# Ratings inside the last projection groups, weights behind the gather indices, and six filler matmuls

## The chip, the cores and the metric

One core of a Trainium2 chip runs the whole program. The metric is the device time of one execution in microseconds. Before the change it is 911.22 us, the median of 3 runs (910.05 to 912.13).

## What is computed

One decoder layer for 512 prompt tokens and 8 sample tokens (520 rows of 1024 columns, float32). Three sublayers follow one another, each with a residual and a layer normalization:

```python
hp = layer_norm(ALPHA * hp + mix_p, ln1_g[l], ln1_b[l])                      # linear attention + latent attention
hp = layer_norm(ALPHA * hp + cross_attention(hp, mk_p, mv_p, w_xq[l], w_xo[l]), ln2_g[l], ln2_b[l])
hp = layer_norm(ALPHA * hp + hier_moe(hp, *moe_w), ln3_g[l], ln3_b[l])

def hier_moe(h, w_grp, b_grp, w_rtr, b_rtr, w_e_gate, w_e_up, w_e_down):
    grp_logits = jnp.einsum('td,dg->tg', t, w_grp)            # 4 groups
    g_idx = jnp.argmax(grp_logits + b_grp, axis=-1)
    e_logits = jnp.einsum('td,de->te', t, w_rtr)              # 32 experts, 8 in a group
    _, top_i = lax.top_k(in_grp + in_bias, TOP_K_IN_GROUP)    # two experts of the token's group
    ...
    for e in range(N_EXPERTS):
        he = jax.nn.silu(t @ w_e_gate[e]) * (t @ w_e_up[e])
        y = y + gates[:, e:e + 1] * (he @ w_e_down[e])
```

The change lies between the second sublayer's output projection (`w_xo`) and the first expert pair of the third.

## The kernel before, in words

**Rows and names.** The 520 rows are tiles 0 to 3 of 128 rows and tile 4, the 8 sample rows. `out_proj("wxo", ...)` multiplies by `w_xo` in four column quarters q; `natural` (L422 on) runs, for each q, first the sample rows, then tiles 0 to 3. One tile of one quarter is a *group* of 24 matmuls (8 k times the three products of a split float32). After a group `put` adds the residual and takes statistics on VectorE; after q = 3 `put` calls `finish(t)`, which normalizes the tile (`normalize`: aggregate, square root on ScalarE, reciprocal, one 1024-column subtract-and-multiply), stores it to `h2d` in DRAM from the SP queue, and enters the tile's *rating* as a stream.

**Rating.** `rate(t)` transposes the normalized tile (8 PE transposes, L223, into `psm`), copies the two halves out on ScalarE and VectorE, and after a pause multiplies by the router weights (16 PE instructions into `pss`), then adds biases on VectorE.

**Order of PE.** `keep_in_program_order` pins TensorE to the order in which the text emits matmuls. That order comes from `Streams.run`: the live generators are sorted by priority; the first whose due time has come runs to its next `yield`. Time there is `PE.now`, the planner's own estimate: 0.123 for a matmul of a projection group (2.94 for a group), 0.11 for a transpose, 0.06 for a router matmul. A rating has priority -1, so it goes first whenever its due time is reached at a `yield`. The projection yields once at the end of each group. The order of VectorE, ScalarE, SP and POOL is drawn up by a list scheduler from priorities (program order) and readiness; `tc.high_priority(offset=...)` moves instructions forward in it.

**The step to the experts.** When the last group is out, `second` closes the pool of the split weights and opens `arena_l` in its place; `prefetch` then issues one DMA of 512 KB (`in_we`) for every free block of 1024 columns. A block comes free again when `gate_up` has used it (`drop`, after every second k); the first two that come free go to `sums` for other use. After the ratings of all five tiles VectorE finds group and two experts for each token (`first_max`), PE counts ranks (`pp`, then `placed`), and VectorE makes the row index of each expert slot (`ixg`, L1834 and L1835). POOL gathers the rows of the first two expert pairs by it (indirect DMA from `h2d`, L1841). Behind the gathers stand `grank` (rank in the group) and, in `weigh`, the gate weights and the group places; `weigh` is called inside `gate_up(0)`. `warm(2)` puts two 512-column float32 matmuls on PE ahead of `turn(0)`, which transposes the gathered rows; `gate_up(0)` follows, then the 15 other pairs. Each expert has 3 MB of weights, 100.7 MB in all.

Of the kernel before, what the change touches and what calls it, by code (L numbers as in the profile page):

```python
# [16 lines left out]
AF = mybir.ActivationFunctionType  # L17
OP = mybir.AluOpType
AX = mybir.AxisListType
# [16 lines left out]
PRIO = 300  # L36
# [262 lines left out]
def tile_hybrid_decoder_step(ctx: ExitStack, tc: tile.TileContext, a):  # L299
    nc = tc.nc  # L300
    PE = Tensor(tc, nc.tensor)
    Q = Loads(PE, nc.sync)
    V, S, G = Engine(PE, nc.vector, 1.05e-3), Engine(PE, nc.scalar, 0.83e-3), Engine(PE, nc.gpsimd, 2.25e-3)
# [42 lines left out]
    streams = Streams(PE)  # L346
# [69 lines left out]
    def natural(name, parts, x, xs, put, ks=range(8), tiles=range(4), need=None):  # L416

        for q in range(parts):  # L420
            ws = {}
            for k in ks:  # L422
                if k // 4 not in ws:
                    ws[k // 4] = yield from weight(a[name][q, k // 4], xs is not None)
            done.add((name, q))
            if xs is not None:
                if need and q == 0:
                    yield need(4)
                ps = pd()
                for i, k in enumerate(ks):  # L430
                    PE.matmul(ps[32 * (i % 4):32 * (i % 4) + NS, :256], xs[:, k],
                              ws[k // 4][2][:, (k % 4) * 256:(k % 4) * 256 + 256], start=i < 4, stop=i >= 4,
                              abreast=4)
                raws.extend(w[2] for w in ws.values())
                put(4, q, ps)
            for t in tiles:
                if need and q == 0:
                    yield need(t)
                ps = pd()
                for i, k in enumerate(ks):  # L440
                    w = [v[:, (k % 4) * 256:(k % 4) * 256 + 256] for v in ws[k // 4][:2]]
                    mm3(ps[:, :256], *x(k, t), *w, i == 0, i == 7)
                put(t, q, ps)
                yield PE.now
            for w in ws.values():
                release(w)
# [897 lines left out]
    def normalize(t, parts):  # L1344
        y, n = res[t], tiles5[t][1]
        mv, rs = moments(t, parts)
        V.tensor_scalar(y[:n], y[:n], mv[:n, 0:1], rs[:n], op0=OP.subtract, op1=OP.mult)
# [304 lines left out]
    def rate(t):  # L1652

        o, n = tiles5[t]
        slots = moe["xt"].slots
        if not slots:
            yield lambda: slots
        h2T = slots.pop(0)
        for c in range(2):
            ps = pm()  # L1660
            for k in range(4):
                f = 4 * c + k
                PE.transpose(ps[:, k * 128:k * 128 + n], res[t][:n, f * 128:(f + 1) * 128], ident[:n, :n])
            to, p3 = h2T[:, 4 * c:4 * c + 4, :n], ps.rearrange("p (k n) -> p k n", k=4)[:, :, :n]
            if c:
                V.tensor_copy(to, p3)
            else:
                S.copy(to, p3)
        yield PE.ready()
        ps = ps_()  # L1670
        for k in range(8):
            PE.matmul(ps[:n, :36], h2T[:, k, :n], moe["wrt"][:, k], start=k == 0, stop=k == 7)
        V.tensor_add(biased[:n, t], ps[:n, :36], moe["bias2"][:n])
        V.tensor_add(logits[:n, t], ps[:n, :36], moe["bias"][:n])
        slots.append(h2T)
        done.add(("rated", t))
# [3 lines left out]
    def second():  # L1680
        yield after("cross queries")

        def finish(t):
            o, n = tiles5[t]
            normalize(t, 4)
            Q.dma_start(h2d[o:o + n, :], res[t][:n])
            streams.add(rate(t), -1, PE.now + 3.8)

        yield from out_proj("wxo", columns2(hh, hl), xs, range(8), finish, lambda t: crossed)
        AF_.free(raws, xs)  # L1690
        pre.close()
        late = ctx.enter_context(tc.tile_pool(name="late", bufs=1, side="right", reuse_waits="tile"))
        AF_.more.more = Arena(late.tile([128, COLS_L], F32, name="arena_l"), COLS_L)
        moer = ctx.enter_context(tc.tile_pool(name="moer", bufs=1, side="right", reuse_waits="tile"))
        AM = Arena(moer.tile([128, COLS_M], F32R, name="arena_m"), COLS_M)
        moe["oh"], moe["yh"] = Ring(AM, 2, GC), Ring(AM, 2, 2, D)
        prefetch()
        yield after(*(("rated", t) for t in range(5)))
        AF_.free(res)
        moe["sums"] = [AF_.get(D) for _ in range(2)]  # L1700
        prefetch()
# [43 lines left out]
    BC = [128, 5]  # L1745
# [34 lines left out]
    el = logits[:, :, 4:36]  # L1780
    eb4 = biased[:, :, 4:36].rearrange("p t (g e) -> p t g e", g=4)
    pp = pm()
    OH = []
    og4 = None
    for k in range(2):
        o = first_max(eb4, 4, 8)
        if og4 is None:
            og = first_max(biased[:, :, None, 0:4], 1, 4)
            og4 = og.rearrange("p t o g -> p t (o g)")[:, :, :, None].to_broadcast(BC + [4, 8])
# [12 lines left out]
    pos = pp[:, :160].rearrange("p (t e) -> p t e", t=5)  # L1802
    rank = R(2, keep=True)
    VAL, RR = [R(2, 4, 16, dt=BF) for _ in range(2)], []
    t32 = R(32)
    ps = pm()
# [25 lines left out]
        placed(ps, k, val, k == 0, k == 1)  # L1832
    ixg = M([16], I32, keep=True)
    V.tensor_scalar(ixg, ps[:, :16], BIG, None, op0=OP.add)  # L1834
    V.tensor_tensor(ixg, ixg, ps[:, 16:32], op=OP.add)  # L1835


    xgs, ohr, yhr, iota = (moe[n] for n in ("xg", "oh", "yh", "iota"))
# [9 lines left out]
    for pr in range(2):  # L1848
# [1 line left out]


    grank = R()
    V.tensor_tensor(t32.rearrange("p t (g e) -> p t g e", g=4), og4, pos.rearrange("p t (g e) -> p t g e", g=4),
                    op=OP.mult)
    V.reduce_sum(grank, t32, axis=AX.X)
    V.tensor_scalar(grank, grank, 0.5, None, op0=OP.mult)

    OHS, YH, HT = {}, {}, {}

    def warm(n):  # L1860

        ps = px()
        for _ in range(n):
            PE.matmul(ps, ident, iota[:, :512], start=True, stop=True)
# [134 lines left out]
        Q.dma_start(v, a["lnr"][i:i + 1].to_broadcast([128, D]))  # L1999
        last.append(v)  # L2000

    warm(2)
    turn(0)
    vv, gate, gslot, over = R(2, keep=True), M([16], keep=True), M([16], keep=True), M([1], I32, 1, True)
    gix = M([2, 4], I32, keep=True)
# [1 line left out]
    def weigh():  # L2007

        gl_ = logits[:, :, 0:4]
        m0, gs, pg, ge = R(), R(), R(), R(4)  # L2010
        V.reduce_max(m0, gl_, axis=AX.X)
        V.tensor_tensor(ge, gl_, m0[:, :, None].to_broadcast(BC + [4]), op=OP.subtract)
        S.activation(ge, ge, AF.Exp)
        V.reduce_sum(gs, ge, axis=AX.X)
        V.reciprocal(gs, gs)
        V.tensor_mul(ge, ge, og.rearrange("p t o g -> p t (o g)"))
        V.reduce_sum(pg, ge, axis=AX.X)
        V.tensor_mul(pg, pg, gs)
        for k in range(2):
            V.tensor_mul(t32, OH[k], el)  # L2020
            V.reduce_sum(vv[:, :, k], t32, axis=AX.X)
        V.reduce_max(m0, vv, axis=AX.X)
        V.tensor_tensor(vv, vv, m0[:, :, None].to_broadcast(BC + [2]), op=OP.subtract)
        S.activation(vv, vv, AF.Exp)
        V.reduce_sum(gs, vv, axis=AX.X)
        V.reciprocal(gs, gs)
        V.tensor_mul(gs, gs, pg)
        V.tensor_tensor(vv, vv, gs[:, :, None].to_broadcast(BC + [2]), op=OP.mult)
        vp = R(2, 4, dt=BF)
        V.tensor_scalar(vp[:, :, :, 3], grank[:, :, None].to_broadcast(BC + [2]), 255.0, -256.0, op0=OP.min, op1=OP.add)  # L2030
        rest = vv
# [6 lines left out]
        ps = ps_()  # L2038
# [210 lines left out]
```

## Time and profile before

| | us |
|---|---|
| median of 3 runs | 911.22 |
| the profiled execution's own time | 907.26 |
| its span | 905.5 |
| last projection quarter and ratings | 597.2 to 623.1 |
| choice of experts, to the row index | 623.2 to 632.4 |
| first expert pair's first matmul | 639.6 |
| DMA queue full | from 648 to 870 |
| end of the last expert and output | 870 to 905.5 |

The times inside the span come from one profiled execution, counted from its start. It is 3.96 us under the median of the runs. A row of the timeline merges neighbouring instructions of one form: its first number is the start, its second the time from the first start to the last end. PE is the matmul engine, PEld its weight loads, DVE VectorE, ACT ScalarE, POOL GpSimd, SPq the SP queue's DMA issues.

### The profile page before, as it was taken

What the parts mean: (1) busy time and instruction counts of PE and PEld (TensorE: products, weight loads), DVE (VectorE), ACT (ScalarE), POOL (GpSimd) and SP (SyncE); (2) the same over time, 40 slices, a digit from 0 to 9 for tenths busy, and PEclk for the clock granted to TensorE, in tenths of its full rate; (3) what the DMA queues carried; (4) which work ended last, traced back from release to release, by engine and by line L of the source; (5) the groups of instructions that cost most, each with busy time, mean ns of one, the idle gap of its engine ahead of it and who ended that gap; (6) DMA issues with size and microseconds to landing.
All of it is one profiled execution on the core that took longest, in us unless ns stands there. A gap on an engine that the chain in (4) does not pass through costs nothing.

```text
span 905.5 us, 17155 instructions
## 1 busy us (share of the span) xinstructions
PE 820.4 (91%) x6767; PEld 575.3 (64%) x6767; DVE 485.7 (54%) x1079; ACT 294.4 (33%) x616; POOL 87.5 (10%) x88
## 2 busy tenths in 40 slices
PE   6999989999997898999989989996899989989982
PEld 6998556666875786898768965995343434334331
DVE  5565356675557554533651675567453834625635
ACT  5422334352632433420442342121232403313311
POOL 4100101111320000000000001000310210200100
PEclk9999999999997987999979999998899999989997
DMA  7922696766793576688867346228699999999950
GB/s 265 310 80 79 178 281 203 247 196 230 231 350 132 192 256 233 228 307 318 268 218 278 98 162 209 84 107 313 209 409 411 412 409 410 408 409 409 409 210 24
DMA packets 83960, 230.43 MB, mean 254 GB/s; under 512 B 12482, under 2 KB 32988, under 8 KB 83492
## 3 DMA queue, kind: packets, MB, share of 16 engines
q1 hardware_dynamic: 74660, 203.98, 62.7%
q0 software_dynamic: 9216, 25.31, 8.0%
q8 instruction: 55, 0.90, 0.4%
q14 instruction: 29, 0.24, 0.1%
HBM read 223.11 MB, written 14.39 MB: 262 GB/s over the span
## 4 chain that ended last, share of the span: by engine, by line
PE 62%; DMA 22%; DVE 8%; ACT 3%; issue 2%; SPq 2%; POOL 0%; POOLq 0%; ACTq 0%; DVEq 0%
PE psd L219 33%; DMA arena_f<-in_we 10%; PE psm L219 9%; PE psx L219 9%; PE pss L219 7%; DVE arena_f L200 5%; DMA arena_d<-in_we 4%; PE psm L223 3%; DMA arena_l<-in_we 2%; DVE arena_r L200 2%; DMA arena_f<-in_latT 2%; ACT arena_f L200 2%; ACT arena_r L200 1%; SPq L239 1%; DMA arena_f<-in_wuq 1%
## 5 line engine op out<-in xcount | busy, mean ns | idle before, releaser
L219 PE MATMUL psd<-arena_r 128*128 128x256 f32 (+1 forms) x2208 | 295.9, 293 | 9.0 <-ACT arena_r L200 5.6
L219 PEld LDWEIGHTS psd<-arena_r 128*128 128x128 f32 x2208 | 281.7, 198 | 21.5 <-issue 9.3
L219 PE MATMUL psx<-arena_f 96*32 96x256 f32 (+1 forms) x728 | 132.7, 495 | 2.2 <-DMA arena_f<-in_latT 1.9
L200 DVE TENSOR_TENSOR arena_r<-arena_f,arena_r 128x1024 fp32r<-128x1024 f32 (+3 forms) x71 | 83.0, 1173 | 77.3 <-ACT arena_r L200 71.7
L200 ACT CAST arena_r<-arena_f 128x1024 fp32r<-128x1024 f32 (+3 forms) x73 | 71.2, 977 | 159.2 <-PE psd L219 118.7
L219 PE MATMUL psm<-arena_f 64*32 64x32 f32 (+10 forms) x1394 | 87.1, 282 | 14.4 <-DVE arena_f L200 9.4
L219 PE MATMUL pss<-arena_f 128*8 128x256 f32 (+5 forms) x466 | 92.3, 466 | 1.3 <-ACT arena_f L200 0.7
L219 PEld LDWEIGHTS psx<-arena_f 96*32 96x32 f32 (+1 forms) x728 | 43.9, 125 | 68.5 <-issue 51.9
L223 PE MATMUL psm<-cst,arena_f 128*128 128x128 f32 (+2 forms) x393 | 59.9, 280 | 19.8 <-DVE arena_f L200 5.4
L219 PEld LDWEIGHTS psm<-arena_f 64*32 64x32 f32 (+6 forms) x1384 | 47.6, 123 | 46.2 <-issue 22.5
L223 PEld LDWEIGHTS psm<-cst,arena_f 128*128 128x128 f32 (+2 forms) x393 | 44.0, 148 | 44.1 <-issue 20.4
L200 DVE TENSOR_TENSOR arena_f<-arena_f 128x1024 f32<-128x1024 f32 (+6 forms) x72 | 57.2, 827 | 7.5 <-ACT arena_f L200 3.6
L219 PEld LDWEIGHTS pss<-arena_f 128*8 128x8 f32 (+3 forms) x456 | 30.3, 121 | 37.8 <-issue 26.7
L200 DVE TENSOR_TENSOR arena_f<-arena_f,psx 128x256 f32<-128x256 f32 (+1 forms) x17 | 7.4, 432 | 86.9 <-ACT arena_f L200 86.9
L638 POOL DMA_INDIRECT arena_f<-in_latN,ixn x32 | 34.3, 1073 | 189.9 <-PE psm L219 176.2
L200 DVE SCALAR_TENSOR_TENSOR arena_f<-arena_f,psd 128x256 f32<-128x256 f32 (+2 forms) x60 | 28.6, 489 | 43.9 <-PE psd L219 34.6
L1841 POOL DMA_INDIRECT arena_f<-h2d,arena_s x24 | 26.2, 1092 | 220.8 <-PE psm L223 123.6
L200 ACT ACTIVATE arena_f<-psx 128x256 f32<-128x256 f32 x16 | 6.1, 384 | 122.8 <-PE psx L219 117.5
L219 PE MATMUL psx<-arena_d,arena_f 128*64 128x512 f32 x76 | 37.1, 676 | 9.4 <-DMA arena_d<-in_we 9.4
L219 PE MATMUL pss<-arena_l,arena_f 128*64 128x512 f32 x92 | 43.2, 593 | 0.0
L219 PE MATMUL psx<-arena_l,arena_f 128*64 128x512 f32 x92 | 35.7, 596 | 5.2 <-DMA arena_l<-in_we 5.2
L200 DVE SCALAR_TENSOR_TENSOR arena_m<-pss,arena_s,arena_m 128x512 fp32r<-128x512 f32 x32 | 23.7, 750 | 29.7 <-ACT arena_m L200 29.7
(212 smaller groups left out, 919.8 us busy)
## 6 DMA issues: line engine op xcount, KB each, us to landing
arena_f<-in_we SPq DMA_DIRECT2D x120, 512.0 KB, 10.6
arena_l<-in_we SPq DMA_DIRECT2D x46, 512.0 KB, 10.8
arena_f<-in_latT SPq DMA_DIRECT2D x128, 144.0 KB, 2.9
arena_d<-in_we SPq DMA_DIRECT2D x26, 512.0 KB, 11.1
arena_f<-in_wout SPq DMA_DIRECT2D x16, 512.0 KB, 5.5
arena_f<-in_wxq SPq DMA_DIRECT2D x16, 512.0 KB, 5.4
arena_f<-in_memKT SPq DMA_DIRECT2D x16, 512.0 KB, 5.3
arena_f<-in_memV SPq DMA_DIRECT2D x16, 512.0 KB, 5.2
```

The lines of the kernel that those rows point to most:

```text
L200: return f(out, *args, **kw)
L219: return self.queue(self.eng.matmul(out, lhsT, rhs, **kw))
L223: return self.queue(self.eng.transpose(out, src, ident))
L239: return self.eng.dma_start(out, src)
L638: G.indirect_dma_start(out=out, out_offset=None, in_=src, in_offset=bass.IndirectOffsetOnAxis(ap=ix, axis=0))
L1841: G.indirect_dma_start(out=out, out_offset=None, in_=h2d, in_offset=bass.IndirectOffsetOnAxis(ap=ix, axis=0), bounds_check=NT - 1, oob_is_ ...
```

## The change

It has four parts. The projection yields once more, in the middle of each group of the last quarter. A rating becomes due 2.8 instead of 3.8 planner-us after `finish`, and the normalization of tile 3 gets a higher priority. `grank` and the first part of `weigh` are put, on VectorE, behind the second `ixg` instruction (`issue_after`: order of issue alone, no wait). The fillers ahead of `turn(0)` become six.

```diff
@@ natural @@
                 for i, k in enumerate(ks):
+                    if name == "wxo" and q == 3 and i == 4:
+                        yield PE.now
                     w = [v[:, (k % 4) * 256:(k % 4) * 256 + 256] for v in ws[k // 4][:2]]
@@ second @@
         def finish(t):
             o, n = tiles5[t]
-            normalize(t, 4)
+            with tc.high_priority(offset=PRIO if t == 3 else 0):
+                normalize(t, 4)
             Q.dma_start(h2d[o:o + n, :], res[t][:n])
-            streams.add(rate(t), -1, PE.now + 3.8)
+            streams.add(rate(t), -1, PE.now + 2.8)
@@ the row index @@
-    V.tensor_tensor(ixg, ixg, ps[:, 16:32], op=OP.add)
+    indices = V.tensor_tensor(ixg, ixg, ps[:, 16:32], op=OP.add).ins
@@ grank @@
-    V.tensor_tensor(t32..., og4, pos..., op=OP.mult)
-    V.reduce_sum(grank, t32, axis=AX.X)
-    V.tensor_scalar(grank, grank, 0.5, None, op0=OP.mult)
+    with tc.issue_after(indices):
+        V.tensor_tensor(t32..., og4, pos..., op=OP.mult)
+        V.reduce_sum(grank, t32, axis=AX.X)
+        V.tensor_scalar(grank, grank, 0.5, None, op0=OP.mult)
@@ ahead of turn(0) @@
-    warm(2)
+    warm(6)
     turn(0)
@@ weigh @@
-        V.reduce_max(m0, gl_, axis=AX.X)
-        V.tensor_tensor(ge, gl_, m0[:, :, None].to_broadcast(BC + [4]), op=OP.subtract)
...
-        V.tensor_tensor(vv, vv, gs[:, :, None].to_broadcast(BC + [2]), op=OP.mult)
+        with tc.issue_after(indices):
+            V.reduce_max(m0, gl_, axis=AX.X)
+            V.tensor_tensor(ge, gl_, m0[:, :, None].to_broadcast(BC + [4]), op=OP.subtract)
...
+            V.tensor_tensor(vv, vv, gs[:, :, None].to_broadcast(BC + [2]), op=OP.mult)
```

## Rows read from the trace of the kernel before

**Rows 1.** Stretches: length, busy us (instructions) of PE, PEld, DVE, ACT, POOL; PEclk, DMA share, GB/s

```profile
634.00:636.00 2.00, 1.49 (x2) 0.00 (x0) 1.66 (x9) 0.21 (x1) 1.70 (x2) 0.51 0.44 133
636.00:638.00 2.00, 0.00 (x0) 0.00 (x0) 1.23 (x8) 0.00 (x0) 0.37 (x1) 1.00 0.57 172
...
640.00:644.00 4.00, 4.00 (x14) 1.13 (x12) 2.00 (x9) 2.18 (x3) 0.65 (x1) 0.65 0.25 68
...
660.00:870.00 210.00, 194.40 (x891) 81.01 (x887) 108.72 (x191) 60.33 (x123) 25.76 (x22) 0.98 1.03 410
```

**Rows 2.** SP queue, timeline 612 to 650: weight and tile DMAs as they are issued

```profile
615.12 0.83 SPq L239 DMA_DIRECT2D arena_l<-in_we  x2
619.38 0.33 SPq L239 DMA_DIRECT2D h2d<-arena_f  x1
...
644.83 4.24 SPq L239 DMA_DIRECT2D arena_f<-in_we  x6
```

**Rows 3.** PE timeline 597 to 640: last quarter, ratings, ranks, fillers, first rows

```profile
598.13 6.01 PE L219 MATMUL psd<-arena_r 128*128 128x256 f32 x48
604.08 1.83 PE L223 MATMUL psm<-cst,arena_f 8*128 8x8 f32 x16
...
614.93 1.87 PE L219 MATMUL pss<-arena_s,arena_f 128*128 128x36 f32 x16
616.63 1.07 PE L223 MATMUL psm<-cst,arena_f 128*128 128x128 f32 x8
...
621.16 1.98 PE L219 MATMUL pss<-arena_s,arena_f 128*128 128x36 f32 x16 [0.29 <-ACT arena_f L200]
...
631.22 0.56 PE L219 MATMUL psm<-arena_f,arena_s 128*64 128x32 bf16 x10 [0.55 <-DVE arena_s L200]
631.71 3.78 PE L219 MATMUL psx<-arena_f,cst 128*128 128x512 f32 x4
638.32 1.06 PE L223 MATMUL psm<-cst,arena_f 128*128 128x128 f32 x8 [2.83 <-DMA arena_f<-h2d,arena_s]
```

**Rows 4.** DVE timeline 599 to 619: sample rows normalized, then tile 3

```profile
601.31 0.42 DVE L200 SCALAR_TENSOR_TENSOR arena_f<-arena_f,psd 128x256 f32<-128x256 f32 x1
...
602.54 0.80 DVE L200 TENSOR_SCALAR arena_f<-arena_f,mv,lrs 8x1024 f32<-8x1024 f32 x1
...
615.12 0.42 DVE L200 SCALAR_TENSOR_TENSOR arena_f<-arena_f,psd 128x256 f32<-128x256 f32 x1 [1.97 <-PE psd L219]
615.58 0.43 DVE L200 BATCH_NORM_STATS2 arena_s<-arena_f 128x6 f32<-128x256 f32 x1
...
618.54 0.81 DVE L200 TENSOR_SCALAR arena_f<-arena_f,mv,lrs 128x1024 f32<-128x1024 f32 x1
```

**Rows 5.** DVE timeline 631 to 635: around the row index

```profile
631.98 0.32 DVE L200 TENSOR_TENSOR arena_f<-arena_s 128x160 f32<-128x160 bf16 x1
632.22 0.17 DVE L200 TENSOR_TENSOR arena_s<-arena_s,psm 128x16 int32<-128x16 int32 x1
...
632.64 1.48 DVE L200 TENSOR_TENSOR arena_f<-arena_f 128x1280 bf16<-128x1280 f32 x1
```

**Rows 6.** POOL timeline 633 to 637, and the chain's wait for the first gather

```profile
633.15 1.92 POOL L1841 DMA_INDIRECT arena_f<-h2d,arena_s  x1 [74.60 <-DMA arena_f<-in_we]
635.38 0.99 POOL L1841 DMA_INDIRECT arena_f<-h2d,arena_s  x1 [0.30 <-issue]
...
633.15 5.04 DMA arena_f<-h2d,arena_s
```

**Rows 7.** All row gathers from `h2d`, the view of that tile

```profile
DMA to landing us min/median/max: 2.9/7.4/10.4
```

**Rows 8.** PEld timeline: some weight loads of the first `gate_up`

```profile
639.56 0.29 PEld L219 LDWEIGHTS psx<-arena_f 128*64 128x64 f32 x4 [0.41 <-ACT arena_f L200]
...
642.17 0.24 PEld L219 LDWEIGHTS psx<-arena_f 128*64 128x64 f32 x2 [0.62 <-issue]
...
643.35 0.14 PEld L219 LDWEIGHTS psx<-arena_f 128*64 128x64 f32 x2 [0.29 <-issue]
643.77 0.14 PEld L219 LDWEIGHTS psx<-arena_f 128*64 128x64 f32 x2 [0.29 <-issue]
```

More of the change, by code (lines that the diff above doesn't have):

```diff
@@ L1852, in tile_hybrid_decoder_step @@
     grank = R()
-    V.tensor_tensor(t32.rearrange("p t (g e) -> p t g e", g=4), og4, pos.rearrange("p t (g e) -> p t g e", g=4),
-                    op=OP.mult)
-    V.reduce_sum(grank, t32, axis=AX.X)
-    V.tensor_scalar(grank, grank, 0.5, None, op0=OP.mult)
+    with tc.issue_after(indices):
+        V.tensor_tensor(t32.rearrange("p t (g e) -> p t g e", g=4), og4, pos.rearrange("p t (g e) -> p t g e", g=4),
+                        op=OP.mult)
+        V.reduce_sum(grank, t32, axis=AX.X)
+        V.tensor_scalar(grank, grank, 0.5, None, op0=OP.mult)
     OHS, YH, HT = {}, {}, {}
@@ L2010, in weigh @@
         m0, gs, pg, ge = R(), R(), R(), R(4)
-        V.reduce_max(m0, gl_, axis=AX.X)
-        V.tensor_tensor(ge, gl_, m0[:, :, None].to_broadcast(BC + [4]), op=OP.subtract)
[L2013 to L2027, printed above, removed]
-        V.tensor_tensor(vv, vv, gs[:, :, None].to_broadcast(BC + [2]), op=OP.mult)
+        with tc.issue_after(indices):
+            V.reduce_max(m0, gl_, axis=AX.X)
+            V.tensor_tensor(ge, gl_, m0[:, :, None].to_broadcast(BC + [4]), op=OP.subtract)
+            S.activation(ge, ge, AF.Exp)
+            V.reduce_sum(gs, ge, axis=AX.X)
+            V.reciprocal(gs, gs)
+            V.tensor_mul(ge, ge, og.rearrange("p t o g -> p t (o g)"))
+            V.reduce_sum(pg, ge, axis=AX.X)
+            V.tensor_mul(pg, pg, gs)
+            for k in range(2):
+                V.tensor_mul(t32, OH[k], el)
+                V.reduce_sum(vv[:, :, k], t32, axis=AX.X)
+            V.reduce_max(m0, vv, axis=AX.X)
+            V.tensor_tensor(vv, vv, m0[:, :, None].to_broadcast(BC + [2]), op=OP.subtract)
+            S.activation(vv, vv, AF.Exp)
+            V.reduce_sum(gs, vv, axis=AX.X)
+            V.reciprocal(gs, gs)
+            V.tensor_mul(gs, gs, pg)
+            V.tensor_tensor(vv, vv, gs[:, :, None].to_broadcast(BC + [2]), op=OP.mult)
         vp = R(2, 4, dt=BF)
```

## The prediction, made before the changed kernel had run

> **What bounds the kernel now.** I read the stretches first, then the SP queue, then back through PE and VectorE. From 660 to 870 us the DMA share is 1.03 at 410 GB/s [rows 1]: the expert weights arrive as fast as the queue moves them, and PE waits for them at the end. The last expert's work after 870 is the same in both kernels. So the end of the run is fixed by when that stream gets going, and the reader is to look at where it last paused. Between 634 and 648 it did: 133, 172 and 68 GB/s [rows 1]. SP's next weight block leaves at 644.83 us [rows 2], because every free block is filled and another comes free only when the first `gate_up` has used k = 0 to 3 (the first two blocks to come free go to `sums`). What moves that 644.83 moves the end of the run by as much; what does not move it is worth nothing.
>
> The chain to 644.83 runs: last router product of tile 3 on PE, to 623.14; VectorE's choice of experts, with PE's rank products to 631.78; fillers to 635.49; the first gathered rows' transposes from 638.32 [rows 3], released by the gather that POOL started at 633.15 and that landed 5.04 us later [rows 6]; `gate_up` from 639.56 [rows 8].
>
> **Part 1, ratings among the groups.** PE is nearly full from 598.13 to 623.14 [rows 3], so an exchange of order there can win only PE's idle time, two pauses of 0.29 like the one in the row of 621.16 and little else. What counts is whether the new order makes PE wait. I followed the planner by hand, with its own prices: a group is 2.94, and `finish(4)` comes with the sample rows, at time S. Before, the sample rating is due at S + 3.8, which falls inside the second group, so its transposes stand behind tiles 0 and 1; the rows show them there, at 604.08. Now it is due at S + 2.8, and tile 0's group ends at S + 2.94: its transposes stand right behind tile 0. Continuing, I get the order: tile 0, transposes of 4, tile 1, transposes of 0, half of tile 2, router product of 4, transposes of 1, the other half, products of 0 and 1, tile 3, transposes of 2 and 3, products of 2 and 3.
>
> On the chip tile 0 ends at 598.13 + 2.98 = 601.1 (two groups take 5.95 from start to start). The sample rows are normalized only at 602.54 + 0.80 = 603.34 [rows 4]. PE's order is pinned, so it stands 2.3 us, and all groups behind it wait. From there: transposes of 4 to 603.85, tile 1 to 606.8, transposes of 0 (0.95; eight of them take 1.07 with the tail) to 607.75, half a group to 609.25, product of 4 to 610.05 (0.8, an estimate between nothing and the 1.7 of a full one), transposes of 1 to 611.0, half a group to 612.5, two products at 1.7 (614.93 to 616.63) to 615.9, tile 3 to 618.9. Transposes of 2 need 0.95. Those of tile 3 need its normalization: 0.42 + 0.43 + 0.81 [rows 4] and three small steps of about 0.3 with their handovers, 2.6 in all; before it took from 615.12 to 619.35, since other work stood between, and the raised priority takes that away. So they start at 621.5, 622.45 ends them, products of 2 and 3 end at 626.0. Against 623.14 that is **2.9 us later**. The bounds: 2.3 less if the sample rows' wait is not there, up to 1.1 under 623.14 if PE never waits.
>
> The pool of split weights closes when tile 3's group is out, so the fill of `arena_l` starts at 618.9 instead of 615.12 [rows 2]. Its blocks must land before the stream's restart, which leaves room (see the rivals).
>
> **Part 2, work behind the index.** Small VectorE steps of `grank` and `weigh` stood among the choice of experts. One is a 0.32 step at 631.98 between the two index instructions; without it the index ends some 0.2 sooner [rows 5]. Ahead of 631.78 the moved ones are mostly small steps that fill latencies between dependent instructions; I give them 0.2 (nothing to 0.5). They reappear behind the index. They are about a dozen steps of the size of 0.17 to 0.32 [rows 5], 2 to 3 us in all. Their readers are PE's gate products, which stand behind `gate_up(0)`; VectorE was busy 1.23 of 2 us from 636 and 2.00 of 4 from 640 [rows 1], so their cost is nothing. Without that cover it would be the 2 to 3 us. ScalarE's two exponentials move with their inputs.
>
> A gather started at 633.15 took 1.92, the next 0.99 [rows 6]; the long one stood beside a 1.48 us VectorE instruction with both inputs in SBUF, from 632.64 to 634.12 [rows 5], and ended 0.95 after it. The Trainium skill (SBUF — State Buffer, section Who interferes with whom) says that such an instruction and a GpSimd instruction that reads SBUF exclude each other, whoever comes first for its whole length. The trace agrees for one instruction; the change puts a row of them exactly behind the index, and by that rule POOL could lose to several in turn and the gather land 2 to 3 us later than with one, at 643 instead of 640.7 below, which would give 914.3 instead of 912.9. The row shows POOL losing once only, and I go by the row.
>
> **Part 3, six fillers.** Two fillers are four PE records. At half clock a record takes 0.87 (639.56 to 642.17 in three steps), at full clock 0.42 (643.35 to 643.77) [rows 8]. Six fillers are twelve: 5.0 us at full clock, 10.4 at half. The granted clock read 0.51 until 636 and 1.00 from there, some 4.3 us after the first filler at 631.71 [rows 1, 3]; then it fell again, and the first `gate_up` ran at 0.65 on average. With 4.3 us at half clock (4.9 records) and 7.1 records at 0.42 the six take 7.3. `turn(0)` stands behind them on PE. They start when the rank products end: 631.78 + 2.9 - 0.2 = 634.5, and end at 641.8, against transposes at 638.32 before. The gather: index at 632.39 + 2.9 - 0.4 = 634.9, POOL 0.76 later (632.39 to 633.15), so 635.7, and landing 5.04 later, 640.7: hidden. The fillers are late next, by about a microsecond.
>
> In return PE stays at full clock: from `turn` to `gate_up` 1.24 as before (its transposes already took 1.06, like the 1.07 at 616.63), then k = 0 to 3, eight steps of 0.43 and the issue, 3.6 instead of 5.27 (639.56 to 644.83).
>
> **The sum.** 641.8 + 1.24 + 3.6 = 646.6 against 644.83: 1.7 us later. The profiled execution's own 907.26 becomes 909.0. The runs' median stands 3.96 above that execution; I put the same shift on it: **912.9**. That is 0.19%, so still "no change" if 0.2% (1.8 us) is about what a measurement of this kernel can tell.
>
> **The rivals.**
>
> *The sample rows' wait does not bite* (the change's first part does nothing): the normalization of 4 is drawn up earlier, or its transposes land behind tile 1 after all. Then 2.3 come off: 910.6. For it: VectorE took up tile 0's residual at 601.31, ahead of the last step of tile 4's normalization [rows 4], an order that a scheduler could turn round. Against: the program up to there is unchanged, and so is what the scheduler sees.
>
> *The ratings do what they say* (faster): PE never waits and the last product ends 1.1 sooner, 622.0. Rank products end at 630.5, fillers at 637.8, `gate_up` starts at 639.0, blocks are issued at 642.6: 2.2 sooner, 909.0. For it: without waits PE's work from 598.13 would allow it. Against: tile 3's normalization alone needs 2.6 behind its group, then 0.95 + 1.7 + 1.7 or more follow.
>
> *The gather lands behind the fillers* (slower). The fill starts 3.8 later and lasts longer into the gather; in a full queue a gather takes 7.4 from issue to landing, alone 2.9 [rows 7]. From 635.7 that is 638.6 to 643.1. It decides from 641.8 on; at 643.1 it adds 1.3: 914.2. For it: the fill before still moved 133 GB/s after 634 [rows 1], with its start at 615.12, and the first gather lost 0.93 (1.92 less 0.99) beside VectorE [rows 6]. Against: SP stood from 615.95 to 619.38 behind tile 3's store [rows 2], and part of that goes.
>
> **How the numbers follow.** Forecast 0.43 (own range 911.6 to 914.2: with the clock rising 1.4 sooner or later the fillers move by 0.7, the small estimates by as much again). No wait 0.21, faster 0.20, late gather 0.16. The forecast's case lies to 0.25 within 0.2% and to 0.18 above it; the no-wait case is within; the late gather above but for 0.02. Faster 0.21, same 0.47, slower 0.32. The range leaves out half of the faster case and the far end of the late gather: 908.6 to 914.8.
>
> **What would show it.** In the trace of the changed kernel: transposes of 4 behind one group, with a PE pause of about 2 us ended by VectorE; tile 3's transposes ahead of the product of tile 2, waiting for VectorE; twelve filler records with the later ones at 0.42; the first `gate_up` at clock 1.00 throughout; SP's first block after the pause near 646.6. If that block comes before 644.8 and the run is not faster, the claim that the stream's restart sets the end is wrong. If PE does not pause at tile 4, the planner was followed wrongly.

## The result, and the profile after

| | before | after |
|---|---|---|
| median of 13 runs each, us | 911.22 | 916.05 |
| ratio, with its 95% interval | 1 | 1.0057 (1.0036 to 1.0077) |
| profiled execution: time; span | 907.26; 905.5 | 914.27; 912.4 |

The changed kernel is about 5 us slower. The forecast was 912.9 with a range up to 914.8: the direction was right, but the time lies above the range.

The PE timeline of the changed kernel (start, us from the first start to the last end, what; in brackets idle time ahead and what ended it) answers to [rows 3]:

```profile
599.67 3.13 PE L219 MATMUL psd<-arena_r 128*128 128x256 f32 x24
605.02 0.63 PE L223 MATMUL psm<-cst,arena_f 8*128 8x8 f32 x8 [2.22 <-DVE lrs L200]
605.58 4.43 PE L219 MATMUL psd<-arena_r 128*128 128x256 f32 x24
...
618.95 3.11 PE L219 MATMUL psd<-arena_r 128*128 128x256 f32 x24
621.90 1.03 PE L223 MATMUL psm<-cst,arena_f 128*128 128x128 f32 x8
624.88 1.06 PE L223 MATMUL psm<-cst,arena_f 128*128 128x128 f32 x8 [1.95 <-DVE arena_f L200]
625.78 5.41 PE L219 MATMUL pss<-arena_s,arena_f 128*128 128x36 f32 x32
...
639.12 0.56 PE L219 MATMUL psm<-arena_f,arena_s 128*64 128x32 bf16 x10 [0.55 <-DVE arena_s L200]
639.62 7.81 PE L219 MATMUL psx<-arena_f,cst 128*128 128x512 f32 x12
647.26 1.04 PE L223 MATMUL psm<-cst,arena_f 128*128 128x128 f32 x8
648.47 7.09 PE L219 MATMUL psx<-arena_f 128*64 128x512 f32 x32 [0.17 <-ACT arena_f L200]
```

The order is the one that the prediction drew up by hand, with its two pauses: 2.22 us ahead of tile 4's transposes and 1.95 us ahead of tile 3's. What the prediction did not have is in the third row: tile 1's group, the same 24 matmuls as tile 0's two rows above, takes 4.43 us instead of 3.13. The two last router products take 5.41; in [rows 3] one takes 1.87 to 1.98. The stretches show the granted clock beside it (columns as in [rows 1]):

```profile
600.00:606.00 6.00, 3.78 (x35) 3.58 (x34) 5.52 (x15) 0.77 (x3) 0.00 (x0) 1.00 0.57 180
606.00:610.00 4.00, 4.00 (x24) 4.00 (x23) 0.00 (x0) 0.00 (x0) 0.00 (x0) 0.61 0.34 134
606.00:607.00 1.00, 1.00 (x10) 1.00 (x9) 0.00 (x0) 0.00 (x0) 0.00 (x0) 0.96 0.43 164
607.00:608.00 1.00, 1.00 (x7) 1.00 (x6) 0.00 (x0) 0.00 (x0) 0.00 (x0) 0.50 0.91 369
610.00:618.00 8.00, 8.00 (x81) 7.80 (x79) 4.83 (x14) 1.68 (x4) 0.00 (x0) 0.98 0.18 68
...
622.00:626.00 4.00, 2.05 (x20) 1.84 (x18) 2.55 (x7) 1.27 (x3) 0.00 (x0) 1.00 0.83 278
626.00:632.00 6.00, 5.20 (x31) 5.06 (x30) 1.74 (x8) 1.47 (x2) 0.00 (x0) 0.62 0.94 326
```

The reader is to look at PEclk: 1.00 in the stretch that holds a pause, 0.61 and 0.62 in the stretch behind it. At a granted clock of 1.00 TensorE runs at 2.4 GHz, at 0.50 at 1.2. The fall comes a little behind the pause: PE is at work again from 605.02, the clock still reads 0.96 from 606 to 607, and 0.50 in the microsecond after that. By these rows each pause is paid twice, first by its length and then by slow work behind it; the experiments put this to the test.

SP's queue, answering to [rows 2]:

```profile
652.15 4.32 SPq L239 DMA_DIRECT2D arena_f<-in_we  x6
```

The first weight block after the pause leaves at 652.15 instead of 644.83, 7.32 later. In this execution everything ahead of the change already ran 1.54 later (tile 0's last group starts at 599.67, not 598.13). I therefore count from the start of that group, here S: block at S + 52.48, before at S + 46.70, so 5.78 later by the change. The span grew by 6.9, which is the 7.32 less the 0.4 by which the stretch from that block to the last `gate_up` was shorter.

POOL, answering to [rows 6]:

```profile
640.88 1.20 POOL L1844 DMA_INDIRECT arena_f<-h2d,arena_s  x1 [80.79 <-DMA arena_f<-in_we]
```

The first gather holds POOL for 1.20 us instead of 1.92. Nothing on PE waits for its rows: `turn` stands right behind the fillers.

### The profile page after: what moved, and what is told of

Read it like the earlier page. It is cut to its first block, busy times and chain, and to the rows that moved or that the text cites. A ratio compares the mean times of both kernels' runs of the same rounds, so it can differ in the third digit from the quotient of the medians.

```text
span 912.4 us, 17171 instructions
## 1 busy us (share of the span) xinstructions
PE 831.9 (91%) x6775; PEld 591.2 (65%) x6775; DVE 486.2 (53%) x1079; ACT 294.2 (32%) x616; POOL 85.8 (9%) x88
## 4 chain that ended last, share of the span: by engine, by line
PE 62%; DMA 23%; DVE 9%; ACT 3%; issue 2%; SPq 1%; POOL 0%; POOLq 0%; DVEq 0%; ACTq 0%
PE psd L219 33%; DMA arena_f<-in_we 11%; PE psm L219 9%; PE psx L219 9%; PE pss L219 7%; DVE arena_f L200 5%; PE psm L223 4%; DMA arena_d<-in_we 3%; DMA arena_l<-in_we 2%; DVE arena_r L200 2%; ACT arena_f L200 2%; DMA arena_f<-in_latT 1%; ACT arena_r L200 1%; DMA arena_f<-in_wuq 1%; DVE arena_s L200 1%
## 5 line engine op out<-in xcount | busy, mean ns | idle before, releaser
L219 PE MATMUL psd<-arena_r 128*128 128x256 f32 (+1 forms) x2208 | 301.8, 296 | 8.8 <-ACT arena_r L200 5.6
L219 PEld LDWEIGHTS psd<-arena_r 128*128 128x128 f32 x2208 | 286.8, 202 | 21.6 <-issue 8.9
L219 PE MATMUL psm<-arena_f 64*32 64x32 f32 (+10 forms) x1394 | 89.1, 282 | 10.8 <-DVE arena_f L200 7.8
L219 PEld LDWEIGHTS psx<-arena_f 96*32 96x32 f32 (+1 forms) x728 | 45.9, 124 | 66.1 <-issue 46.3
L219 PEld LDWEIGHTS psm<-arena_f 64*32 64x32 f32 (+6 forms) x1384 | 49.7, 124 | 42.7 <-issue 22.2
```

The source lines that it names most:

```text
L219: return self.queue(self.eng.matmul(out, lhsT, rhs, **kw))
```

## The experiments

W is the end of the last rank product on PE (639.68 in the changed kernel, 631.78 before). From S to the last router product, from there to W, and from W to SP's first block are the three pieces of the chain. As in the prediction, the first part is the yield in mid-group, the earlier ratings and tile 3's priority together, the second the steps behind the index, the third the six filler pairs. "SP's block" is the first weight block after the pause of the stream. Theory: the pauses of the first part cost their length and the half clock behind them. Rivals: the fillers or the moved steps cost it, or the groups are slow for another reason.

S itself falls between 598.13 and 609.54 in the fourteen profiled executions, though the program ahead of it is the same in all of them. That is more than any of the changes is worth, so the pieces of the chain, each of one execution, are read from S or W, and the intervals of the ratios, some 2 to 3 us to each side, often hold 1 as well as the ratio that was expected.

**1. The first part undone.**

```diff
-                    if name == "wxo" and q == 3 and i == 4:
-                        yield PE.now
...
-            with tc.high_priority(offset=PRIO if t == 3 else 0):
-                normalize(t, 4)
+            normalize(t, 4)
...
-            streams.add(rate(t), -1, PE.now + 2.8)
+            streams.add(rate(t), -1, PE.now + 3.8)
```

> The changed kernel with its first part undone: ratings are queued as in the kernel before; the steps behind the index and the six filler pairs stay. Theory (the loss comes from the two pauses that the ratings put on TensorE, by their length and by the half clock behind them): last router product to SP's first weight block after the pause falls from 21.7 us in the profile before by about 0.6 (the part behind the rank products took 12.47 in the changed kernel against 13.05 before, the choice of experts 8.49 against 8.64), so about 0.7 us faster than before, ratio near 0.999, and faster than the changed kernel by about 6 us. Rival 1 (the six filler pairs are what costs): 1.003 or above, the first block as late behind the rank products as their end plus 14 us or more. Rival 2 (the moved VectorE steps delay the gates or the gather): the gather lands after the fillers' end, ratio above 1.002.

Measured: ratio 1.0010 (0.9981 to 1.0039). The last product comes at S + 25.02 (before 25.01), W 8.48 later (8.64), the block 12.59 behind W (13.05). So parts two and three bring the block forward by 0.6, and the loss of the change is in the first part. The time doesn't show the 0.6: 1 lies inside its interval.

**2. The first part alone,** in the kernel before (the reverse of that diff, with two filler pairs and the steps ahead of the index).

> The kernel before with the first part of the change alone: ratings due earlier, half of tile 2's last group ahead of two products, tile 3's normalization at raised priority; two filler pairs and the steps ahead of the index as before. Theory (the two pauses, 2.2 and 2.0 us, then tile 1's group 1.4 longer and the last two router products 1.9 longer at half clock): the last router product ends some 6 us later than before behind the start of tile 0's group, and the run is 5.5 to 6.5 us slower than before, ratio about 1.0065, a little above the changed kernel's. By my forecast, which counted the pauses alone: 2.9 us, ratio 1.0032. Rival (parts 2 and 3 are what costs): 0 to 1 us, ratio below 1.001.

Measured: 1.0065 (1.0035 to 1.0095). PE timeline:

```profile
608.75 0.63 PE L223 MATMUL psm<-cst,arena_f 8*128 8x8 f32 x8 [2.23 <-DVE lrs L200]
609.31 4.63 PE L219 MATMUL psd<-arena_r 128*128 128x256 f32 x24
...
628.59 1.06 PE L223 MATMUL psm<-cst,arena_f 128*128 128x128 f32 x8 [1.95 <-DVE arena_f L200]
629.49 5.97 PE L219 MATMUL pss<-arena_s,arena_f 128*128 128x36 f32 x32
```

The same two pauses, and behind each the same slow work. The last product ends at S + 32.06, 7.05 later than before. The first part alone is the whole loss and a little more. Which of its three edits does what is not taken apart further, except in experiment 4.

**3. Work in the pauses.** Two filler products ahead of the transposes of tiles 4 and 3, which don't enter the planner's time, so that the order stays:

```diff
         h2T = slots.pop(0)
+        if t in (3, 4):
+            ps = px()
+            for _ in range(2):
+                PE.queue(PE.eng.matmul(ps, ident, moe["iota"][:, :512], start=True, stop=True))
```

> The changed kernel with two filler products (128x512, float32) set ahead of the transposes of tile 4 and of tile 3, so that TensorE works in the two pauses while it waits for the normalizations; the planner's order stays as in the changed kernel. Theory (the clock falls because of the pauses): the transposes start as late as in the changed kernel, or up to 1 us later where the fillers outlast the wait, but tile 1's group takes about 3.0 us again instead of 4.4 and the last two router products about 3.5 instead of 5.3. About 3.3 us faster than the changed kernel, ratio to before about 1.002. Rival (those groups are slow for another reason, such as their operands or a neighbour): the groups stay at 4.4 and 5.3 us, ratio 1.006 or above.

Measured: 1.0028 (1.0003 to 1.0053). PE timeline:

```profile
601.93 1.88 PE L1664 MATMUL psx<-arena_f,cst 128*128 128x512 f32 x4
604.32 0.63 PE L223 MATMUL psm<-cst,arena_f 8*128 8x8 f32 x8 [0.51 <-DVE lrs L200]
604.88 3.14 PE L219 MATMUL psd<-arena_r 128*128 128x256 f32 x24
...
613.24 4.14 PE L219 MATMUL pss<-arena_s,arena_f 128*128 128x36 f32 x32
617.18 5.47 PE L219 MATMUL psd<-arena_r 128*128 128x256 f32 x24
...
626.48 3.77 PE L219 MATMUL pss<-arena_s,arena_f 128*128 128x36 f32 x32
```

The time from tile 0's group to tile 4's transposes is as long as it was (2.22 us from the end of tile 0's group to them), but PE works in it, and tile 1's group is back from 4.43 to 3.14. The two last products are back from 5.41 to 3.77. That is the theory's claim, shown on the same work in the same place. But tile 3's group, 3.11 in the changed kernel, now takes 5.47, and the last product ends at S + 31.28, only 0.24 sooner. So the 1.0028 lies near the expected 1.002 but not for the expected reason: by the chain SP's block comes 5.55 later than before, which would be 1.0061, above the interval. The stretch shows the clock at half there, after PE had worked without any idle time from 604.32 on:

```profile
612.00:616.00 4.00, 4.00 (x38) 4.00 (x36) 1.95 (x6) 0.50 (x2) 0.00 (x0) 1.00 0.23 87
616.00:623.00 7.00, 7.00 (x36) 7.00 (x35) 1.49 (x5) 0.00 (x0) 0.00 (x0) 0.52 0.43 150
```

The clock falls during two router products in a row, 32 matmuls in all, each of 36 columns. Experiment 8 takes this up.

**4. The first pause undone.** The sample rows' rating comes due later. The order behind it moves too: only one router product is left behind the second pause.

```diff
-            streams.add(rate(t), -1, PE.now + 2.8)
+            streams.add(rate(t), -1, PE.now + (5.8 if t == 4 else 2.8))
```

> The changed kernel with the rating of the sample rows (tile 4) due 5.8 instead of 2.8 us behind its normalization, so that its transposes stand behind the second group as before; the other ratings stay at 2.8. Theory (each pause costs its length and the half clock behind it): the first pause, 2.2 us, and the 1.4 us by which tile 1's group was longer are gone, the second pause stays; about 3.6 us faster than the changed kernel, ratio to before about 1.002. By lengths alone: 2.2 us faster than the changed kernel, ratio 1.003. Rival (only tile 3's place at the end matters, work ahead of it is caught up): as the changed kernel, 1.0057.

Measured: 0.9995 (0.9966 to 1.0024). PE timeline:

```profile
604.60 1.83 PE L223 MATMUL psm<-cst,arena_f 8*128 8x8 f32 x16
606.19 3.11 PE L219 MATMUL psd<-arena_r 128*128 128x256 f32 x24
...
621.90 1.20 PE L223 MATMUL psm<-cst,arena_f 128*128 128x128 f32 x8 [1.92 <-DVE arena_f L200]
623.25 3.63 PE L219 MATMUL pss<-arena_s,arena_f 128*128 128x36 f32 x16 [0.16 <-ACT arena_f L200]
```

The group behind the sample rows' transposes takes 3.11. The second pause stays, and the one product behind it takes 3.63 instead of 1.98. The last product ends at S + 28.22, 3.3 sooner than in the changed kernel, where 3.6 was expected (and 2.2 by lengths alone), and SP's block at S + 48.97, 2.27 later than before. By that the ratio should be 1.0025, just above the interval. The time came out better than the chain; no row here shows why.

**5. Four filler pairs,** in the first experiment's kernel (`warm(6)` becomes `warm(4)`).

> The first experiment's kernel (ratings as before, steps behind the index) with four filler pairs instead of six. There the six took 7.94 us, at half clock until 5.1 us after their start; the last two pairs are four records of 0.43, 1.7 us, and the gathered rows are expected about 6 us behind the rank products. Theory (the end of the fillers, not the gather or the clock, is what comes last): transposes start about 5.9 to 6.4 us behind the last rank product instead of 7.7, the first gate_up still runs at full clock (7.1 us), SP's first block comes 11.0 to 11.5 us behind the rank products instead of 12.6; 1.6 to 2.0 us faster than the kernel before, ratio about 0.998. Rival 1 (the two pairs were holding the clock up): gate_up takes 8 us or more and nothing is won against the first experiment. Rival 2 (the gather comes last): the transposes are released by a DMA at 7 us or later.

Measured: 0.9981 (0.9958 to 1.0005). PE timeline, then the SP queue:

```profile
636.98 5.77 PE L219 MATMUL psx<-arena_f,cst 128*128 128x512 f32 x8
642.58 1.04 PE L223 MATMUL psm<-cst,arena_f 128*128 128x128 f32 x8
643.79 7.09 PE L219 MATMUL psx<-arena_f 128*64 128x512 f32 x32 [0.17 <-ACT arena_f L200]
```

```profile
647.47 4.24 SPq L239 DMA_DIRECT2D arena_f<-in_we  x6
```

W is 637.04. The transposes start 5.54 behind it, no DMA is waited for, `gate_up` still takes 7.09, and the block leaves 10.43 behind W. Six pairs were two more than the clock needed here; both rivals fall. The block is at S + 43.92, 2.78 sooner than before, more than expected; the time's interval still holds 1.

**6. Six filler pairs alone,** in the kernel before (`warm(2)` becomes `warm(6)`).

> The kernel before with six filler pairs instead of two, nothing else. Theory (the fillers cost their end behind the gather and give back the clock of the first gate_up): fillers about 7.8 us, transposes right behind them, gate_up 7.1 us instead of 8.7, SP's first block 12.6 us behind the rank products instead of 13.05; 0.3 to 0.5 us faster than before, ratio 0.9995. Rival (fillers only delay, as they stand ahead of the transposes): 1 us or more slower, ratio 1.001 or above.

Measured: 0.9996 (0.9971 to 1.0021). Fillers 7.99, transposes right behind them, `gate_up` 7.09, block 12.65 behind W: the third part gives back what it takes, to 0.4 us. In the kernel before the first `gate_up` ran at 0.65 between 640 and 644 [rows 1].

**7. The steps behind the index alone,** in the kernel before (the two `with tc.issue_after(indices)` of the change).

> The kernel before with the weights' and group places' steps issued behind the index, nothing else. Theory: the index ends 0.2 us sooner behind the rank products (0.43 instead of 0.61), the choice of experts 0.1 to 0.2 sooner; POOL's first gather takes 1.2 us as in the changed kernel instead of 1.92, so that the rows land up to 0.9 us sooner, and PE waits for them behind two filler pairs as before: 0.3 to 1.2 us faster than before, ratio 0.9987 to 0.9997. Rival (the steps behind the index hold up the copies of the transposes or the gather): SP's first block 13.05 us or more behind the rank products, ratio 1.0 or above.

Measured: 0.9986 (0.9957 to 1.0016). PE timeline, POOL, and a stretch:

```profile
638.64 1.94 PE L223 MATMUL psm<-cst,arena_f 128*128 128x128 f32 x8 [1.79 <-DMA arena_f<-h2d,arena_s]
640.51 9.25 PE L219 MATMUL psx<-arena_f 128*64 128x512 f32 x32
```

```profile
634.34 1.21 POOL L1841 DMA_INDIRECT arena_f<-h2d,arena_s  x1 [74.26 <-DVE arena_s L200]
```

```profile
640.00:645.00 5.00, 5.00 (x15) 1.58 (x15) 3.82 (x19) 2.21 (x6) 0.99 (x1) 0.51 0.22 58
```

W is 633.15; the gathered rows release PE 5.49 behind it, not 6.54 as in [rows 3] (638.32 less 631.78). This 1 us does not reach SP's block: it leaves at 646.36, 13.21 behind W, since the clock stayed at half here and `gate_up` took 9.25. The block thus came as late as the rival wanted it, but not by the rival's way: the gather came sooner, not later. The theory's path was right, its gain went to the clock.

**8. Work between the router products too.** The third experiment's kernel with a filler product ahead of the router products of tiles 0 and 1:

```diff
         yield PE.ready()
+        if t in (0, 1):
+            ps = px()
+            PE.queue(PE.eng.matmul(ps, ident, moe["iota"][:, :512], start=True, stop=True))
```

> The third experiment's kernel (two filler products in each of the two pauses) with one more filler product ahead of the router product of tile 0 and one ahead of that of tile 1. There the clock fell to half while PE worked without a pause, during the two router products of 36 columns in a row, and tile 3's group took 5.47 us instead of 3.11. Theory (those narrow products themselves let the clock fall): with the fillers between them it holds, tile 3's group takes 3.1 us, the two products and the fillers take about 5.4 (3.7 and twice 0.85); the last router product ends 29.8 to 30.2 us behind the start of tile 0's group instead of 31.3, and a run about 1 us faster than the third experiment. Rival (something else drops it, such as a neighbour or a fixed rhythm): tile 3's group stays at 5 us or more and the last product ends 32 us or later.

Measured: 1.0055 (1.0025 to 1.0086). PE timeline:

```profile
618.26 1.10 PE L1678 MATMUL psx<-arena_f,cst 128*128 128x512 f32 x2
619.20 1.87 PE L219 MATMUL pss<-arena_s,arena_f 128*128 128x36 f32 x16
620.90 3.11 PE L219 MATMUL psd<-arena_r 128*128 128x256 f32 x24
...
626.84 1.06 PE L223 MATMUL psm<-cst,arena_f 128*128 128x128 f32 x8 [0.23 <-DVE arena_f L200]
627.74 3.66 PE L219 MATMUL pss<-arena_s,arena_f 128*128 128x36 f32 x32
```

```profile
616.00:623.00 7.00, 7.00 (x53) 6.16 (x52) 2.49 (x9) 0.29 (x1) 0.00 (x0) 1.00 0.46 150
```

Tile 3's group is at 3.11, and no stretch from S to the last product is under a clock of 1.00. The last product ends at S + 29.98, as expected. Of that, 1.7 us are the two added fillers (from the first of them to tile 3's group 615.70 to 620.90, 5.20; the same products in the changed kernel 615.46 to 618.95, 3.49), so the first part without half clock ends at S + 28.3, 3.3 later than before; the changed kernel's 31.52 is 3.2 more. That splits its 6.5 us: **3.3 for the pauses' lengths, 3.2 for the clock behind them** (3.2 in that execution; by 32.06 and 31.92 in experiments 2 and 11 it was 3.6 to 3.8). The time, however, is not better than the third experiment's 1.0028, though the block comes 2.1 sooner by the chain, where 1 us of gain was expected. So the split is shown in the chain of the profiles, not in the times.

**9. Four filler pairs alone,** in the kernel before (`warm(2)` becomes `warm(4)`).

> The kernel before with four filler pairs instead of two, nothing else. With the steps behind the index too, four pairs brought SP's first block 10.4 us behind the rank products (13.05 before), the fillers ended 5.8 us behind them and no DMA was waited for. Without those steps the gather landed 6.4 us behind the rank products in the kernel before, and 5.5 with them in the run of that part alone. Theory (with four pairs the gather comes last, so that the second part is now worth what the gather gains): the transposes are released by a DMA at 6.3 to 6.5 us, SP's first block comes about 11.3 us behind the rank products, 1.7 us faster than before, ratio 0.998; about 0.9 us more than with the steps behind the index. Rival (the fillers end last here too): no wait for a DMA, 10.4 to 10.6 us, and the second part is worth nothing even here.

Measured: 0.9977 (0.9950 to 1.0003). PE timeline and POOL:

```profile
644.60 1.06 PE L223 MATMUL psm<-cst,arena_f 128*128 128x128 f32 x8 [1.49 <-DMA arena_f<-h2d,arena_s]
```

```profile
639.17 1.93 POOL L1841 DMA_INDIRECT arena_f<-h2d,arena_s  x1 [74.61 <-DMA arena_f<-in_we]
```

W is 637.79. With four pairs PE does wait for the gather, to 6.81 behind W, a little later than expected, and the block leaves 11.72 behind W; with the steps behind the index it was 10.43. So the second part is worth 1.3 us of the chain where the gather ends last, and nothing beside six pairs.

**10. The fifth kernel again.**

> The kernel of the fifth experiment once more (ratings as before, steps behind the index, four filler pairs), on the same chip as the four pairs alone. Expected as there: SP's first block 10.4 us behind the rank products, 1.5 to 2.8 us faster than the kernel before, ratio 0.997 to 0.9985. If the ratio is 1.0 or above, the earlier one was chance.

Measured: 0.9992 (0.9965 to 1.0020). The chain repeats (10.50 behind W, S + 43.99), but the ratio is outside what I expected. Twice below 1, with 1 inside both intervals: by the times it isn't shown to be faster than the kernel before.

**11 and 12. The changed kernel and the eighth experiment's, side by side.**

> The changed kernel itself once more, beside the next one on the same chip. Expected: 1.005 to 1.006, as before; in the profile again two TensorE pauses of about 2 us and half clock behind each of them, with the last router product 31.3 to 31.8 us behind the start of tile 0's last group.

> The eighth experiment's kernel (fillers in the pauses and between the router products) once more, beside the changed kernel. By its profile SP's first block came 50.2 us behind the start of tile 0's group, against 52.5 in the changed kernel and 46.7 in the kernel before; so 2.3 us faster than the changed kernel, ratio to the kernel before 1.0035 to 1.004. Its times gave 1.0055 then, and the third experiment's, with a slower stage in the profile, 1.0028. If it comes out at 1.0055 again, beside a changed kernel that is no slower, the gain of the stage in the profile doesn't reach the time.

Measured: changed 1.0079 (1.0044 to 1.0114), the other 1.0062 (1.0030 to 1.0093). Both are above what was expected. The changed kernel shows the same pauses, tile 1's group at 4.63, the last two products at 5.84, their end at S + 31.92, SP's block at S + 52.42. The other's last product ends at S + 29.98 again, to the hundredth. But behind W it differs from its own first profile: fillers 8.10 us instead of 7.08, block 12.76 behind W instead of 11.73. And the end differs. First the row of the PE timeline that begins the last expert's `gate_up`, of the eighth experiment and of the twelfth:

```profile
876.23 0.64 PE L219 MATMUL psx<-arena_d,arena_f 128*64 128x512 f32 x1 [2.04 <-DMA arena_d<-in_we]
```

```profile
877.03 0.85 PE L219 MATMUL psx<-arena_d,arena_f 128*64 128x512 f32 x1 [2.06 <-DMA arena_d<-in_we]
```

Then of each, in the same order, a stretch and that `gate_up` as a step of the chain of waits (start, us, what):

```profile
877.00:881.00 4.00, 4.00 (x20) 1.29 (x18) 0.00 (x0) 0.00 (x0) 0.00 (x0) 1.00 0.39 155
```

```profile
876.23 6.65 PE psx L219 x29
```

```profile
877.00:881.00 4.00, 3.97 (x12) 1.25 (x14) 0.00 (x0) 0.00 (x0) 0.00 (x0) 0.57 0.60 240
```

```profile
877.03 8.35 PE psx L219 x29
```

This step comes after the stream. PE waits as long for the last blocks in both executions; behind the wait the clock stays up in one and falls in the other, and the step takes 6.65 or 8.35 us. One kernel can do either, so 2.7 us between these two profiles (1.0 behind W, 1.7 at the end) are no difference of kernels. That is about the gain of 2.3 that these two runs were to show, and the times leave it open.

The pieces of the chain side by side (us, from the PE timelines and SP queues):

| kernel | last product, from S | W to SP's block | SP's block, from S | last `gate_up` | ratio |
|---|---|---|---|---|---|
| before | 25.01 | 13.05 | 46.70 | 6.65 | 1 |
| changed | 31.52 | 12.47 | 52.48 | 6.65 | 1.0057 |
| 1, parts two and three | 25.02 | 12.59 | 46.09 | 8.33 | 1.0010 |
| 2, part one | 32.06 | 12.80 | 53.49 | 8.35 | 1.0065 |
| 3, work in the pauses | 31.28 | 12.48 | 52.25 | 6.65 | 1.0028 |
| 4, sample rows later | 28.22 | 12.27 | 48.97 | 6.65 | 0.9995 |
| 5, four pairs | 25.01 | 10.43 | 43.92 | 8.35 | 0.9981 |
| 6, six pairs alone | 25.01 | 12.65 | 46.30 | 6.65 | 0.9996 |
| 7, behind the index alone | 25.01 | 13.21 | 46.70 | 6.65 | 0.9986 |
| 8, and between the products | 29.98 | 11.73 | 50.19 | 6.65 | 1.0055 |
| 9, four pairs alone | 25.02 | 11.72 | 45.37 | 6.65 | 0.9977 |
| 10, four pairs again | 25.01 | 10.50 | 43.99 | 8.35 | 0.9992 |
| 11, changed again | 31.92 | 12.02 | 52.42 | 6.65 | 1.0079 |
| 12, as 8 again | 29.98 | 12.76 | 51.23 | 8.35 | 1.0062 |

## Why the prediction was wrong

**The bound: right.** From SP's first block to the start of the last `gate_up` it takes 225.17 us before and 224.76 after, and between 224.4 and 225.3 in all the kernels above. Within a profiled execution, what moves the block moves the end one to one, except for the clock at the very end. The medians follow the chain less closely: in experiments 3 and 4 they are about 3 us better than it.

**The order and both pauses: right.** Tile 4 waits 2.22 (forecast 2.3); tile 3 waits for its normalization, 1.95 of idle time behind the transposes of tile 2. The rival in which the sample rows' wait does not bite falls with the first, the one in which the ratings do what they say with both.

**The step that failed** is "From there: ... tile 1 to 606.8" and on to "products of 2 and 3 end at 626.0": every instruction behind the two pauses was priced at the durations of [rows 3], which were taken at full clock (granted 1.00 all through the last quarter of the kernel before). The last product was to come 2.9 later. It came 6.51 later (31.52 against 25.01): 3.3 by length, where the mechanism and nearly the size were right (tile 4's transposes came 5.35 behind the start of tile 0's group instead of 5.2, tile 3's 5.93 behind the start of their group instead of 5.6), and 3.2 because TensorE ran at half clock behind each pause. Tile 1's group alone took 1.3 more, the last two products 1.75 more (5.41 against 3.66 in experiment 8). The trace of before had shown it, in a stretch that I did not hold against the first part:

```profile
626.00:632.00 6.00, 2.38 (x31) 1.79 (x31) 5.70 (x28) 0.00 (x0) 0.00 (x0) 0.50 1.03 416
```

There PE had stood since its last product at 623.14. The prediction counted with the clock in the third part and not in the first. For the same reason the range was too narrow: its upper end had a late gather, but no price for a slow TensorE behind the waits that it forecast itself. The Trainium skill (TensorE: Matmul & The Clock Gate, section HAM oscillation — how this bites in real kernels) describes waits that let the clock fall, so that the work behind each starts slow. The trace agrees on the fall, by the 4.43 of tile 1's group against the 3.14 when PE works in the pause; but that work did not start slow, the clock read 0.96 from 606 to 607 and fell behind that.

**The second part: right in what it does.** The choice of experts took 8.49 instead of 8.64, and the index ended 0.43 behind W instead of 0.61 (forecast 0.2 each). The fear that POOL would lose to several VectorE steps in a row did not come true: the gather took 1.20, less than before. The long VectorE step now starts at 641.12, behind the gather's start at 640.88; before it stood ahead of it [rows 5, 6]. With the moved steps the gather takes 1.20 and 1.21 in experiments 5 and 7, without them 1.92 and 1.93 in experiments 6 and 9. By the rule of the Trainium skill (SBUF — State Buffer, section Who interferes with whom) the first comer goes first and the other is blocked. For the gather the trace agrees; the VectorE step, now the second comer, takes 1.49 against 1.48 before, so no wait of it shows.

**The third part: right.** W to the transposes took 7.58 (forecast 7.3), from there to `gate_up` 1.21 (1.24), to the block 3.68 (3.6). The late gather falls as a rival: PE waits for no DMA ahead of the transposes, and in experiment 7 the rows were there 5.49 behind W, under the fillers' 7.58.

**The sum.** The block was to come 1.7 later and came 5.78 later. Of the 4.1 between, 3.6 is the first part (6.51 less 2.9) and 0.4 what stands behind W; the index's share is 0.05. The shift to the median did not hold: the profiled execution of after lies 1.78 under its median, not 3.96 as the one of before. The profiled execution missed its forecast by 5.3 us (914.27 against 909.0: the 4.1, and 1.5 from ahead of S, less 0.4), the median by 3.1, and that the second miss is the smaller one is luck. Two slips in the working changed nothing: the gather at 643 would give 914.1, not 914.3, and the chances add up to 0.20 for faster and 0.48 for the same, not 0.21 and 0.47. That a gather alone takes 2.9 and in a full queue 7.4 is a reading of the least and the median in [rows 7], which the row doesn't show.

## What to carry to other kernels

A wait put on TensorE costs its length, and it can cost the half clock of the work behind it: price what stands behind the wait at both clocks, and look in the trace of before for pauses of that size and the granted clock after each. Here the pauses of 1.92 to 2.23 us among the groups were followed by half clock in each of the four profiles that have them, a wait as long ahead of the last `gate_up` in five of fourteen. Where TensorE is nearly full, a new order of its work can gain little more than its idle time, here two pauses of 0.29 us, but it can lose the pauses it makes and the clock behind them. Where fillers hold the clock, compare their end with the data that the next step waits for: in the chain of the profiles four pairs gave the first `gate_up` the same clock as six, 2.2 us sooner.

## What the runs showed that I had not expected

The clock can fall without a pause: in experiment 3 it fell during two router products of 36 columns, with PE busy throughout, and with a filler ahead of each of them it stayed up in both profiles (experiments 8 and 12; 5.47 without and 3.11 with them for the group behind). Experiment 3 has one profile alone. In the changed kernel the same two products stood in a row and the clock held (0.98 from 610 to 618), so they alone don't decide it, and what does is open.

Two profiled executions of one kernel (experiments 8 and 12) had the clock rise and fall at other places: fillers of 7.08 and 8.10 us, a last `gate_up` of 6.65 and 8.35. Each of these is worth 1 to 1.7 us, of the size of most differences tried here. In all fourteen profiles PE waits 1.96 to 2.12 us for the last blocks just ahead of the last `gate_up`; in nine the clock stays at 1.00 behind that wait, in five it reads 0.50 within about 1 us of its end. So a wait of this length does not always bring the clock down, and the traces here don't show what decides it. The long form of the last `gate_up` stands in the profiles of experiments 1, 2, 5, 10 and 12. Three of these have their block sooner than before and two later, so I do not call it a consequence of either. For the gains of experiments 5 and 10 it took back 1.7 of 2.7 us in the profiled executions; whether it does so in most executions is open.
